# Block 14's halves copied on ScalarE behind the last one-hots; power ahead of the second gather; ranks, search steps, picks and weight parts at other steps

## The chip, the cores and the metric

The kernel runs on one core of a Trainium2 chip. The metric is device time in microseconds (us); the kernel before takes 1840.52 us (median of three runs, 1840.33 to 1842.64). The engines are TensorE (PE; PEld is its weight load), VectorE (DVE), ScalarE (ACT), GpSimd (POOL) and SyncE (SP), which only issues DMAs here. Each runs its instructions in program order and waits on semaphores for the others.

## The reference

```
lat = lat + g1 * ((gate_b * conv3(gate_c * v)) @ w_out)     # gate_b, gate_c, v = split(hl @ w_in)
h   = modulate(rms_norm(lat, norm_g[1]), sh2, sc2)          # 2048 tokens x 1024
aff = softmax(h @ w_router)                                 # 16 experts
g, idx = top_k(aff.T, 256)                                  # expert choice: 256 tokens an expert
hid = silu(h[idx] @ w_gate[e]) * (h[idx] @ w_up[e])
lat = lat + g2 * scatter_add(idx, (hid @ w_down[e]) * g)
```

There is one layer, in float32; a condition vector gives the shifts, scales and gates (sh, sc, g1, g2).

## The kernel before

All large products are split: each operand is rounded to a high part (`fp32r`) and a low part, the remainder, and PE adds three products (high x high, high x low, low x high). Of every weight piece of 512 KB, `split_high` (ACT, L267, 1.05 us) makes the high part and `split_low` (DVE, L277, 1.22 us) the low one; raw pieces come on SP's queue, and a raw buffer's next load is issued when its low part is done.

Tokens are worked on in 16 blocks of 128. Up to about 530 us the kernel computes the conditioning, the norm, the in-projection and the convolution. Then each block tb goes through the out-projection: eight steps k of `out_mm(tb + 1, k)` (L1217, L1218, L1220), and behind each step `behind(tb, k)` issues work of earlier blocks: residual and norm (`out_res`, L1232 and L1234), the second norm's output (`out_h2`, L1315), its transfer to memory as two 16-bit halves (`halves_out`, L1286), from which a DMA transpose makes the router's operand, the router's products (`router_mm`, `router_sum` L1387, for the last blocks `turn_xt` L1330 and `direct_mm` L1339), and the softmax (`router_sm`, L1397 to L1407).

In the same stretch the first expert's 256 tokens are found by ranks, so that its gather can begin before the last block is done. For block c, `row_turn` (L1445) turns its affinities into a row, `rank_a` compares it with all rows so far (`hits`, DVE L1456, and `equal`, POOL L1459 and L1460), `rank_b` counts on PE (L1466), and `rank_c` (DVE L1471) corrects the counts. After blocks 7 and 11 the ranked tokens are sorted and cut to 256 (`sort_a` L1475 and L1477, `sort_b` L1489, `sort_c`, `sort_d`, and a turn of `best`). `plan` lists at which (block, step, order within the step) each of these runs; steps with a negative third number run ahead of `behind_block`, the others after it. All the small PSUM tiles of these functions come from one pool, `tp`, which has two buffers that are handed out in turn; an allocation waits until the last reader of the tile two allocations earlier is done.

The last block (730 to 747 us) is written out by hand. `fetch_first` gathers the ranked tokens (POOL L1627, two gathers), `out_res_last` and `out_rms` norm the block (the power, POOL L1270), the softmax gives its affinities (logits L1399), PE turns `best` into a row (L1642) and the block's own values into another (L1654), DVE counts (L1657 to L1666) and makes the one-hots `chosen` (L1669, L1671), PE picks the columns of the first expert's operand (L1686, L1688) and turns the rest (L1693). `fill(n)` issues n matmuls whose result is not used. Block 14's halves are copied by POOL (L1284) and stored from POOL's queue (L1288).

The experts follow in the order gate_up(0), down(0), gate_up(1), down(1), gate_up(2), and from then on gate_up(e) and down(e - 1) by halves. A gate_up half has 8 steps k of 24 products of 256 columns (L1908), a down half 4 steps kk of 12 products of 512 columns (L1995 to L1997). Places are written (stage, expert, half, step, i): i = -1 is ahead of the weight splits of the step, 0 behind them, 1 in the middle of its products. The tables `SPLITS`, `HIGH`, `DOWN_SPLITS` and `DOWN_HIGH` say up to which weight piece low parts are made in a step and how many high parts more. `FEW_AT` places the rounds of the search for the threshold of expert 1 (PE L382 behind DVE L379), `ALL_AT` those for all experts (counts DVE L1713 and ACT L1717, PE L1724, DVE L1726 and L1730; one step joins the key's two parts, L1800), and `PICK_AT` the picks of experts 1 to 3: `pick_oh` makes one-hots (DVE L1821), `pick` multiplies them (PE L1829), copies the result out (DVE L1831) and gathers the tokens (POOL L1837); experts 1 and 2 are turned on PE by `turn_here` (L1879, its copies L1881 and L1882). After a gate_up half, ACT and DVE form the gated products (L1938, L1939, L1942).

Of the kernel before, what the change touches and what calls it, by code (L numbers as in the profile page):

```python
# [13 lines left out]
ALU = mybir.AluOpType  # L14
# [4 lines left out]
D = 1024  # L19
# [20 lines left out]
SPLITS = {(0, 0): (0, 1, 2, 3, 4, 6, 8, 10), (0, 1): (10, 11, 12, 13, 14, 15, 16, 18),  # L40
          (1, 0): (25, 27, 28, 29, 30, 32, 33, 34), (1, 1): (34, 35, 37, 38, 39, 40, 40, 41),
          (2, 0): (51, 52, 54, 55, 55, 57, 59, 60), (2, 1): (61, 62, 63, 64, 65, 67, 68, 69)}
HIGH = {(0, 0): (2, 2, 2, 2, 2, 2, 1, 1), (0, 1): (1, 1, 1, 1, 1, 1, 1, 1),
        (1, 0): (0, 0, 1, 0, 0, 0, 0, 0)}
DOWN_SPLITS = {(0, 0): (19, 19, 20, 21), (0, 1): (22, 24, 25, 25),
               (1, 0): (42, 43, 44, 46), (1, 1): (47, 48, 49, 50)}
DOWN_HIGH = {(0, 0): (1, 1, 1, 1), (0, 1): (1, 1, 1, 1),
             (1, 0): (1, 1, 1, 1), (1, 1): (1, 1, 1, 1)}
# [4 lines left out]
          ("g", 0, 1, 5, 1)]  # L53
ALL_AT = [("d", 0, 0, 1, 0), ("d", 0, 0, 2, 1), ("d", 0, 0, 3, 1), ("d", 0, 1, 0, 1), ("d", 0, 1, 1, 1),
# [3 lines left out]
PICK_AT = {1: (("g", 0, 1, 6, 0), ("g", 0, 1, 7, 0), ("d", 0, 0, 3, 0), ("d", 0, 1, 0, 0),  # L58
# [14 lines left out]
def block_kernel(ctx: ExitStack, tc, x, c, ada_w, ada_b, norm_g, w_in, conv, w_out, router, wg, wu, wd, out):  # L73
# [330 lines left out]
    with tc.tile_pool(name="mix", bufs=1) as mix, ExitStack() as ctx_mixd:  # L404
# [839 lines left out]
        def out_res_last(tb):  # L1244
# [7 lines left out]
            direct_mm(tb, 0)  # L1252
            pt = turn_xt(tb, 1, True, lambda: fill(2))
            fill(2)
            nc.vector.tensor_tensor(ss[:, 0:1], ss[:, 1:2], ss[:, 2:3], op=ALU.add)
            for j in (0, 2):
                nc.vector.tensor_copy(hx_of[tb][:, 4 + j:6 + j], pt[:, j:j + 2])
                if j == 0:
                    nc.vector.tensor_scalar(ss[:, 1:2], ss[:, 3:4], ss[:, 0:1], 1.0 / D, op0=ALU.add, op1=ALU.mult)
# [162 lines left out]
        def value(c, n=1):  # L1422
            return affh[:, c // 8, 0, c % 8:c % 8 + n]
# [85 lines left out]
        def plan():  # L1509
            for c, t, a, b, d in ((0, (5, 7), (6, 4), (6, 7), (6, 7, 6)), (1, None, (6, 7), (7, 3), (7, 4)),  # L1510
# [6 lines left out]
                early = -4 if c == 11 else 0  # L1517
                if t:
                    steps[(*t, 7)] = lambda c=c: row_turn(place(c), value(c, 1 if c else 4))
# [591 lines left out]
```

## Time and profile before

| | |
|---|---|
| median of three runs | 1840.52 us |
| profiled execution | 1838.64 us |
| its span | 1836.9 us |
| mean granted TensorE clock | 0.997 |

The profile is one execution. Its page gives the busy time of each engine, the queues, the chain that ended last and the costliest groups of instructions; the trace behind it can be read as lists of waits, as windows and as a timeline, in us from the span's start. In a timeline a row is: start, length, engine, line, operation, output <- input, shape, count; and in brackets the idle time of the engine before it and what released it. The granted clock is 1.00 at 2.4 GHz and 0.50 at 1.2 GHz.

### The profile page before, as it was taken

What the parts mean: (1) busy time and instruction counts of PE and PEld (TensorE: products, weight loads), DVE (VectorE), ACT (ScalarE), POOL (GpSimd) and SP (SyncE); (2) the same over time, 40 slices, a digit from 0 to 9 for tenths busy, and PEclk for the clock granted to TensorE, in tenths of its full rate; (3) what the DMA queues carried; (4) which work ended last, traced back from release to release, by engine and by line L of the source; (5) the groups of instructions that cost most, each with busy time, mean ns of one, the idle gap of its engine ahead of it and who ended that gap; (6) DMA issues with size and microseconds to landing.
All of it is one profiled execution on the core that took longest, in us unless ns stands there. A gap on an engine that the chain in (4) does not pass through costs nothing.

```text
span 1836.9 us, 29869 instructions
## 1 busy us (share of the span) xinstructions
PE 1799.5 (98%) x11588; PEld 1604.7 (87%) x11588; DVE 1282.7 (70%) x1855; ACT 912.0 (50%) x1274; POOL 371.0 (20%) x579
## 2 busy tenths in 40 slices
PE   7999999999999999999999999999999999999997
PEld 6788888887888777889899999999999999999996
DVE  6786878888867776777676666676576566666653
ACT  4665455333445554655465455455455445545541
POOL 2324201121111645222200210211121021021102
PEclk9999999999999999999999999999999999999999
DMA  9756565565589774666787887978878878787774
GB/s 338 245 174 212 170 227 183 161 162 136 147 259 293 222 212 146 232 184 198 222 257 218 256 233 224 265 214 243 261 225 238 241 252 230 230 255 227 234 225 81
DMA packets 306494, 401.09 MB, mean 218 GB/s; under 512 B 100004, under 2 KB 170960, under 8 KB 306352
## 3 DMA queue, kind: packets, MB, share of 16 engines
q1 hardware_dynamic: 280736, 307.91, 54.9%
q0 software_dynamic: 25616, 91.26, 17.0%
q8 instruction: 91, 1.49, 0.3%
q14 instruction: 51, 0.42, 0.1%
HBM read 316.27 MB, written 63.98 MB: 207 GB/s over the span
## 4 chain that ended last, share of the span: by engine, by line
PE 85%; DVE 6%; DMA 2%; ACT 2%; issue 2%; POOL 1%; SPq 0%; POOLq 0%; DVEq 0%; ACTq 0%
PE pm L1908 38%; PE pm L1995 6%; PE pm L1997 6%; PE pm L1996 6%; PE pm L920 5%; PE pm L922 5%; PE pm L921 5%; PE pm L1217 2%; PE pm L1218 2%; PE pm L1220 2%; PE pm L546 1%; PE pm L547 1%; PE pm L549 1%; DMA rows<-aw 1%; DVE sb L900 1%
## 5 line engine op out<-in xcount | busy, mean ns | idle before, releaser
L1908 PE MATMUL pm<-xT,ws 128*128 128x256 f32 x6144 | 712.2, 278 | 0.0
L1908 PEld LDWEIGHTS pm<-xT,ws 128*128 128x128 f32 x6144 | 708.9, 188 | 2.9 <-DVE ws L277 0.4
L277 DVE TENSOR_TENSOR ws<-raw,ws 128x1024 fp32r<-128x1024 f32 x389 | 462.4, 1221 | 259.3 <-ACT ws L267 259.1
L267 ACT ACTIVATE ws<-raw 128x1024 fp32r<-128x1024 f32 x389 | 393.7, 1053 | 386.9 <-PE pm L1908 271.2
L2031 POOL DMA_INDIRECT out_dram<-ot,idx x30 | 96.6, 3220 | 544.5 <-DVE ot L2020 540.5
L1995 PE MATMUL pm<-ws,hT 128*128 128x512 f32 x504 | 199.5, 396 | 0.0
L1997 PE MATMUL pm<-ws,hT 128*128 128x512 f32 x504 | 198.6, 394 | 0.0
L1996 PE MATMUL pm<-ws,hT 128*128 128x512 f32 x504 | 197.4, 392 | 0.0
L920 PE MATMUL pm<-tg,sb 128*128 128x512 f32 x472 | 184.7, 391 | 1.1 <-ACT cx L987 1.1
L922 PE MATMUL pm<-tg,sb 128*128 128x512 f32 x472 | 183.8, 389 | 0.0
L921 PE MATMUL pm<-tg,sb 128*128 128x512 f32 x472 | 183.7, 389 | 0.0
L900 DVE TENSOR_TENSOR sb<-raw,sb 128x512 fp32r<-128x512 f32 x144 | 98.9, 689 | 59.1 <-ACT sb L899 57.8
L899 ACT ACTIVATE sb<-raw 128x512 fp32r<-128x512 f32 x144 | 88.7, 625 | 65.7 <-DVE raw L908 14.6
L1997 PEld LDWEIGHTS pm<-ws,hT 128*128 128x128 f32 x504 | 95.0, 188 | 20.3
L1996 PEld LDWEIGHTS pm<-ws,hT 128*128 128x128 f32 x504 | 95.0, 188 | 19.6
L1995 PEld LDWEIGHTS pm<-ws,hT 128*128 128x128 f32 x504 | 94.9, 188 | 18.6
L920 PEld LDWEIGHTS pm<-tg,sb 128*128 128x128 f32 x472 | 88.6, 188 | 19.6 <-ACT cx L987 1.5
L922 PEld LDWEIGHTS pm<-tg,sb 128*128 128x128 f32 x472 | 88.6, 188 | 18.6
L921 PEld LDWEIGHTS pm<-tg,sb 128*128 128x128 f32 x472 | 88.6, 188 | 18.2
L1217 PE MATMUL pm<-ws,hl 128*128 128x512 f32 x256 | 104.2, 407 | 0.0
L1218 PE MATMUL pm<-ws,hl 128*128 128x512 f32 x256 | 100.0, 390 | 0.0
L1837 POOL DMA_INDIRECT xs<-hhalf,idx x26 | 37.8, 1456 | 260.1 <-issue 194.1
(453 smaller groups left out, 2365.6 us busy)
## 6 DMA issues: line engine op xcount, KB each, us to landing
raw<-in_moe_w_gate_dram SPq DMA_DIRECT2D x128, 512.0 KB, 5.0
raw<-in_moe_w_up_dram SPq DMA_DIRECT2D x128, 512.0 KB, 4.4
raw<-in_moe_w_down_dram SPq DMA_DIRECT2D x128, 512.0 KB, 4.6
raw<-in_sc_w_in_dram SPq DMA_DIRECT2D x42, 512.0 KB, 4.7
aw<-in_ada_w_dram POOLq DMA_DIRECT2D x32, 512.0 KB, 5.1
xt<-in_x_dram SPq DMA_DIRECT2D x31, 512.0 KB, 5.9
fu<-fscr SPq DMA_DIRECT2D x23, 512.0 KB, 4.9
hl<-in_ada_w_dram SPq DMA_DIRECT2D x32, 256.0 KB, 6.8
```

What stands on the lines that cost most here:

```text
L267: nc.scalar.activation(t[:, 0], raws[n_high], AF.Copy)
L277: (eng or nc.vector).tensor_sub(t[:, 1, ..., s], raw[..., s], t[:, 0, ..., s].bitcast(F32))
L900: nc.vector.tensor_sub(t[:, 1], full, t[:, 0].bitcast(F32))
L920: nc.tensor.matmul(o, t[:, 0, j], r[:, 0], start=(first and j == 0), stop=False, skip_group_check=True)
L921: nc.tensor.matmul(o, t[:, 1, j], r[:, 0], start=False, stop=False, skip_group_check=True)
L922: nc.tensor.matmul(o, t[:, 0, j], r[:, 1], start=False, stop=end, skip_group_check=True)
L1217: nc.tensor.matmul(ps[h], vh[:, k], w[:, 0, half(h)], start=(k == 0), stop=False)
L1218: nc.tensor.matmul(ps[h], vh[:, k], w[:, 1, half(h)], start=False, stop=False)
L1908: nc.tensor.matmul(o, w[:, i // 2, j, c0], xT[:, i % 2, k], start=(k == i == 0 and f % 2 == 0), stop=(k == KD - 1 and i == 2), skip_group_ ...
L1995: nc.tensor.matmul(ps[s], h, w[:, 0, j], start=(k == 0), stop=False)
L1996: nc.tensor.matmul(ps[s], h, w[:, 1, j], start=False, stop=False)
L1997: nc.tensor.matmul(ps[s], l, w[:, 0, j], start=False, stop=(k == KD - 1))
```

## The change

In the last block, `direct_mm(tb, 0)` takes the place of the filler between the two pairs of transposes, the second gather is issued behind the power and the sum of the sorted values, two fillers are shorter, and block 14's halves are copied on ScalarE and stored from SP's queue; the copy's place in program order stays behind the one-hots. The ranks and sorts get tables of places of their own, and several functions may share a place. The searches, the picks and the weight parts get other places in their tables.

```diff
-SPLITS = {(0, 0): (0, 1, 2, 3, 4, 6, 8, 10), (0, 1): (10, 11, 12, 13, 14, 15, 16, 18),
-          (1, 0): (25, 27, 28, 29, 30, 32, 33, 34), (1, 1): (34, 35, 37, 38, 39, 40, 40, 41),
+SPLITS = {(0, 0): (0, 1, 2, 3, 5, 7, 8, 10), (0, 1): (10, 10, 11, 12, 14, 15, 16, 19),
+          (1, 0): (25, 27, 28, 29, 29, 30, 32, 33), (1, 1): (34, 35, 37, 38, 39, 40, 40, 41),
...
-        (1, 0): (0, 0, 1, 0, 0, 0, 0, 0)}
...
+        (1, 0): (1, 2, 2, 1, 1, 1, 1, 2), (1, 1): (2, 1, 0, 0, 0, 0, 0, 0),
...
-               (1, 0): (42, 43, 44, 46), (1, 1): (47, 48, 49, 50)}
...
+               (1, 0): (45, 46, 46, 48), (1, 1): (50, 51, 51, 52)}
...
-          ("g", 0, 1, 5, 1)]
+          ("g", 0, 1, 7, -1)]
...
-          ("g", 1, 0, 1, -1), ("g", 1, 0, 2, -1), ("g", 1, 0, 3, -1), ("g", 1, 0, 4, -1), ("g", 1, 0, 4, 0),
-          ("g", 1, 0, 5, 0), ("g", 1, 0, 7, -1), ("g", 1, 1, 1, -1), ("g", 1, 1, 2, -1), ("g", 1, 1, 3, -1),
-          ("g", 1, 1, 4, -1), ("g", 1, 1, 4, 1), ("g", 1, 1, 5, -1), ("g", 1, 1, 5, 1), ("g", 1, 1, 6, -1)]
...
-           2: (("g", 1, 1, 7, 0), ("d", 1, 0, 0, 0), ("d", 1, 0, 3, -1), ("d", 1, 1, 0, -1),
-               ("d", 1, 1, 1, -1), ("d", 1, 1, 1, -1)),
...
+          ("g", 1, 0, 1, -1), ("g", 1, 0, 2, -1), ("g", 1, 0, 2, 1), ("g", 1, 0, 3, -1), ("g", 1, 0, 4, -1),
+          ("g", 1, 0, 4, 1), ("g", 1, 0, 6, 0), ("g", 1, 1, 1, -1), ("g", 1, 1, 2, -1), ("g", 1, 1, 3, -1),
+          ("g", 1, 1, 4, -1), ("g", 1, 1, 4, 1), ("g", 1, 1, 5, -1), ("g", 1, 1, 5, 0), ("g", 1, 1, 6, 0)]
...
+           2: (("g", 1, 1, 7, 1), ("g", 1, 1, 7, 1), ("d", 1, 0, 2, -1), ("d", 1, 0, 3, 1),
+               ("d", 1, 1, 1, 0), ("d", 1, 1, 1, 0)),
...
+RANK_AT = {0: ((5, 7, 7), (6, 0, 3), (6, 6, 3), (6, 7, 3)),
...
+           4: ((6, 7, 5), (8, 0, 0), (8, 6, 0), (8, 7, 3)),
+           5: ((7, 7, -3), (8, 7, 0), (9, 4, 3), (9, 5, 0)),
+           6: ((8, 7, 7), (9, 0, 3), (9, 6, 0), (9, 7, 5)),
+           7: ((10, 0, -3), (10, 2, -3), (10, 6, 5), (10, 7, -1)),
+           8: ((10, 7, 7), (11, 7, 3), (12, 1, -3), (12, 2, 2)),
+           9: ((11, 7, 5), (12, 4, 0), (12, 5, 6), (12, 6, 3)),
...
+SORT_AT = {7: ((11, 2, 0), (11, 5, -3), (11, 6, -3)),
+           11: ((13, 0, -0.5), (13, 4, -1), (13, 6, 3))}
...
             fill(4)
-            direct_mm(tb, 0)
-            pt = turn_xt(tb, 1, True, lambda: fill(2))
+            pt = turn_xt(tb, 1, True, lambda: direct_mm(tb, 0))
             fill(2)
...
-            for c, t, a, b, d in ((0, (5, 7), (6, 4), (6, 7), (6, 7, 6)), (1, None, (6, 7), (7, 3), (7, 4)),
...
-                                  (4, (6, 7), (8, 4), (8, 7), (8, 7, 6)), (5, (7, 7), (8, 7), (9, 3), (9, 4)),
-                                  (6, (8, 7), (9, 4), (9, 7), (9, 7, 6)), (7, (9, 7), (10, 4), (10, 7), (10, 7)),
...
+            for c, (t, a, b, d) in RANK_AT.items():
...
-                    steps.pop(t)()
+                    for f in steps.pop(t):
+                        f()
...
         fetch_first(1)
-        fetch_first(0)
         out_res_last(tb)
         out_rms(tb)
         sort_v(pk_c)
+        fetch_first(0)
...
-        fill(6)
+        fill(4)
...
-        fill(7)
+        fill(6)
...
-        halves_out(tb - 1, u_last[0], eng=nc.gpsimd)
+        halves_out(tb - 1, u_last[0])
```

In `RANK_AT` the four places of a block are those of `row_turn`, `rank_a`, `rank_b` and `rank_c`; in `SORT_AT` the three are those of `sort_a`, of `sort_b` with `sort_c` and `sort_d`, and of the turn of `best`.

## Rows read from the trace of the kernel before

**Rows 1.** The page's first part: busy time of each engine, its share of the span, and instructions.

```profile
PE 1799.5 (98%) x11588; PEld 1604.7 (87%) x11588; DVE 1282.7 (70%) x1855; ACT 912.0 (50%) x1274; POOL 371.0 (20%) x579
```

**Rows 2.** The list of PE's waits: tile and line, what released it, then us in total, times, and the longest.

```profile
PE pt L1879 <- DMA xs<-hscr,idx: 3.4, 1, 3.4
...
PE pc L1724 <- ACT hit L1717: 2.4, 1, 2.4
```

**Rows 3.** Windows: stretch, its length, busy time and instructions of PE, PEld, DVE, ACT and POOL, the granted clock, the share of the DMA engines and GB/s. The stretches are that of the last one-hots, that behind a search round, and that behind the third expert's gather.

```profile
738.00:742.00 4.00, 2.60 (x14) 1.81 (x14) 3.50 (x11) 1.59 (x3) 3.41 (x9) 1.00 0.89 348
...
836.70:839.00 2.30, 2.30 (x13) 2.30 (x13) 1.41 (x2) 1.81 (x2) 0.00 (x0) 0.52 0.56 195
...
883.80:885.00 1.20, 1.19 (x5) 1.20 (x6) 0.00 (x0) 0.06 (x1) 0.00 (x0) 0.50 0.65 249
```

**Rows 4.** The chain that ended last, in order of time: the products of one gate_up half in the later experts.

```profile
1079.45 21.79 PE pm L1908 x192
```

**Rows 5.** The timeline of the last block.

```profile
734.35 0.98 POOL L1627 DMA_INDIRECT xs<-hscr,idx  x1 [0.27 <-POOL idx L1625]
...
735.36 0.87 POOL L1270 TENSOR_TENSOR rstd<-ss,mhalf 128x1 f32<-128x1 f32 x1
...
739.49 0.29 DVE L1669 TENSOR_SCALAR chosen<-slot_r,n_last 128x128 f32<-128x128 bf16 x1
739.54 1.98 POOL L1284 COPY uh<-u 128x2048 uint16<-128x2048 uint16 x1
...
739.88 1.73 DVE L1671 TENSOR_SCALAR chosen<-slot_r,n_last 128x128 f32<-128x128 bf16 x1
...
741.66 0.49 PE L1686 MATMUL pm<-chosen,xs 128*128 128x128 f32 x2 [1.40 <-DVE chosen L1671]
...
745.34 1.04 PE L1693 MATMUL pt<-identf,xs 128*128 128x128 f32 x8
```

**Rows 6.** Two answers on one tile and one line: how long the two gathers of the last block took from issue to landing, and the duration of ScalarE's copies of halves in the earlier blocks (ns, least, median and most).

```profile
DMA to landing us min/median/max: 5.6/6.6/7.7
...
L1286 ACT ACTIVATE hl<-u x14: 1893/1896/1913, 539.0 to 712.8; 128x2048 uint16<-128x2048 uint16 x14
```

**Rows 7.** The timeline of the first gate_up stage, at two rounds of the search for one expert.

```profile
768.68 0.28 PE L382 MATMUL pc<-each,sameq 128*128 128x32 f32 x1 [0.36 <-DVE each L379]
...
775.62 0.28 PE L382 MATMUL pc<-each,sameq 128*128 128x32 f32 x1 [0.68 <-DVE each L379]
```

**Rows 8.** The timeline of the second expert's gate_up, at rounds of the search over all experts: a round's product, its last count, the product that waited, and the products behind it.

```profile
829.19 0.17 PE L1724 MATMUL pc<-cnt,same 128*128 128x4 f32 x1
...
830.91 0.19 ACT L1717 ACTIVATION_READ_ACCUMULATOR hit<-keys,nb 128x1 fp32r x1
...
834.61 0.27 PE L1724 MATMUL pc<-cnt,same 128*128 128x4 f32 x1 [2.40 <-ACT hit L1717]
834.75 4.60 PE L1908 MATMUL pm<-xT,ws 128*128 128x256 f32 x24
```

**Rows 9.** The timeline of the third expert's pick and gather, and, without a time in front, how long from issue to landing the gathers of this expert took and then those of the expert before.

```profile
868.47 2.49 DVE L1821 TENSOR_TENSOR oh<-slot_r,row 128x512 bf16<-128x512 bf16 x4
...
871.48 0.56 PE L1829 MATMUL pi<-ax,oh 128*128 128x10 bf16 x16
...
875.43 0.16 DVE L1831 COPY pk<-pi 128x10 f32<-128x10 f32 x1
...
876.59 1.54 POOL L1837 DMA_INDIRECT xs<-hscr,idx  x1 [19.25 <-DVE gate L1844]
...
878.43 0.96 POOL L1837 DMA_INDIRECT xs<-hscr,idx  x1 [0.30 <-issue]
...
883.82 1.09 PE L1879 MATMUL pt<-identf,xs 128*128 128x128 f32 x4 [3.42 <-DMA xs<-hscr,idx]
...
DMA to landing us min/median/max: 7.1/7.7/8.4
...
DMA to landing us min/median/max: 5.3/5.3/5.3
```

**Rows 10.** The blocks with ranks. First the timeline: starts of a block on VectorE (L1232), the first and the last of the nine places, a compare, the norm's output, and a count on PE. Then a group of instructions by line (busy us, mean ns, idle time before them and its releaser), and, last, who waited for L1471 (us, times).

```profile
601.35 0.68 DVE L1232 TENSOR_TENSOR u<-pm,g1b 128x512 f32<-128x512 f32 x1
...
614.49 0.68 DVE L1232 TENSOR_TENSOR u<-pm,g1b 128x512 f32<-128x512 f32 x1
...
636.97 0.32 PE L1445 MATMUL pt<-identf,aff 128*128 128x128 f32 x1 [0.47 <-DVE aff L1407]
...
642.41 0.68 DVE L1232 TENSOR_TENSOR u<-pm,g1b 128x512 f32<-128x512 f32 x1
...
648.98 1.19 DVE L1456 SCALAR_TENSOR_TENSOR hits<-ranked,zero,aff 128x896 bf16<-128x896 f32 x1
...
650.23 0.30 PE L1466 MATMUL pr<-ones_b,hits 128*128 128x1 bf16 x6
...
651.27 1.41 DVE L1315 SCALAR_TENSOR_TENSOR u<-u,rstd,sh2b 128x512 f32<-128x512 f32 x2
...
679.55 0.32 PE L1445 MATMUL pt<-identf,aff 128*128 128x128 f32 x1 [0.27 <-DVE lg L1397]
...
L1308 DVE TENSOR_TENSOR hl<-hl 128x1024 fp32r<-128x1024 f32 x5 | 6.1, 1226 | 5.9 <-ACT hl L1303 5.9
...
  PE pt L1330: 0.2, 1
```

More of the change, by code (lines that the diff above doesn't have):

```diff
@@ L39 @@
 SORTS = (0, 8, 12)
-SPLITS = {(0, 0): (0, 1, 2, 3, 4, 6, 8, 10), (0, 1): (10, 11, 12, 13, 14, 15, 16, 18),
-          (1, 0): (25, 27, 28, 29, 30, 32, 33, 34), (1, 1): (34, 35, 37, 38, 39, 40, 40, 41),
-          (2, 0): (51, 52, 54, 55, 55, 57, 59, 60), (2, 1): (61, 62, 63, 64, 65, 67, 68, 69)}
-HIGH = {(0, 0): (2, 2, 2, 2, 2, 2, 1, 1), (0, 1): (1, 1, 1, 1, 1, 1, 1, 1),
-        (1, 0): (0, 0, 1, 0, 0, 0, 0, 0)}
-DOWN_SPLITS = {(0, 0): (19, 19, 20, 21), (0, 1): (22, 24, 25, 25),
-               (1, 0): (42, 43, 44, 46), (1, 1): (47, 48, 49, 50)}
-DOWN_HIGH = {(0, 0): (1, 1, 1, 1), (0, 1): (1, 1, 1, 1),
-             (1, 0): (1, 1, 1, 1), (1, 1): (1, 1, 1, 1)}
+SPLITS = {(0, 0): (0, 1, 2, 3, 5, 7, 8, 10), (0, 1): (10, 10, 11, 12, 14, 15, 16, 19),
+          (1, 0): (25, 27, 28, 29, 29, 30, 32, 33), (1, 1): (34, 35, 37, 38, 39, 40, 40, 41),
+          (2, 0): (52, 54, 56, 56, 56, 56, 59, 59), (2, 1): (61, 63, 63, 63, 64, 65, 67, 68)}
+HIGH = {(0, 0): (2, 2, 2, 2, 2, 3, 1, 1), (0, 1): (1, 1, 0, 0, 2, 2, 2, 2),
+        (1, 0): (1, 2, 2, 1, 1, 1, 1, 2), (1, 1): (2, 1, 0, 0, 0, 0, 0, 0),
+        (2, 0): (0, 0, 1, 0, 0, 1, 1, 1), (2, 1): (1, 1, 1, 1, 0, 0, 0, 0)}
+DOWN_SPLITS = {(0, 0): (20, 20, 21, 21), (0, 1): (21, 24, 25, 25),
+               (1, 0): (45, 46, 46, 48), (1, 1): (50, 51, 51, 52)}
+DOWN_HIGH = {(0, 0): (1, 2, 2, 2), (0, 1): (2, 2, 2, 3),
+             (1, 0): (0, 0, 0, 0), (1, 1): (0, 0, 0, 0)}
 N_GROUP = 7
@@ L1251, in out_res_last @@
             fill(4)
-            direct_mm(tb, 0)
-            pt = turn_xt(tb, 1, True, lambda: fill(2))
+            pt = turn_xt(tb, 1, True, lambda: direct_mm(tb, 0))
             fill(2)
             nc.vector.tensor_tensor(ss[:, 0:1], ss[:, 1:2], ss[:, 2:3], op=ALU.add)
[L1256 to L1259, printed above, removed]
+            nc.vector.tensor_copy(hx_of[tb][:, 4:6], pt[:, 0:2])
+            nc.vector.tensor_scalar(ss[:, 1:2], ss[:, 3:4], ss[:, 0:1], 1.0 / D, op0=ALU.add, op1=ALU.mult)
+            nc.vector.tensor_copy(hx_of[tb][:, 6:8], pt[:, 2:4])
         def out_rms(tb):
@@ L1509, in plan @@
         def plan():
-            for c, t, a, b, d in ((0, (5, 7), (6, 4), (6, 7), (6, 7, 6)), (1, None, (6, 7), (7, 3), (7, 4)),
[6 rows of a table removed]
-                early = -4 if c == 11 else 0
-                if t:
-                    steps[(*t, 7)] = lambda c=c: row_turn(place(c), value(c, 1 if c else 4))
-                steps[(*a, 5)] = lambda c=c: rank_a(c)
-                steps[(*b, early + c % 2)] = lambda c=c: rank_b(c)
-                steps[(*d, early + 2 + c % 2) if len(d) == 2 else d] = lambda c=c: rank_c(c)
-            for c, a, b, d in ((7, (11, 2), (11, 4), (11, 6)), (11, (13, 0), (13, 2), (13, 6))):
-                steps[(*a, -0.5 if c == 11 else 4)] = lambda c=c: sort_a(c)
-                steps[(*b, 6)] = lambda c=c: (sort_b(c), sort_d(sort_c()))
-                steps[(*d, 6)] = lambda: row_turn(0, best)
+            for c, (t, a, b, d) in RANK_AT.items():
+                if t:
+                    steps.setdefault(t, []).append(lambda c=c: row_turn(place(c), value(c, 1 if c else 4)))
+                steps.setdefault(a, []).append(lambda c=c: rank_a(c))
+                steps.setdefault(b, []).append(lambda c=c: rank_b(c))
+                steps.setdefault(d, []).append(lambda c=c: rank_c(c))
+            for c, (a, b, d) in SORT_AT.items():
+                steps.setdefault(a, []).append(lambda c=c: sort_a(c))
+                steps.setdefault(b, []).append(lambda c=c: (sort_b(c), sort_d(sort_c())))
+                steps.setdefault(d, []).append(lambda: row_turn(0, best))
         plan()
```

2 lines of the change are left out of this document (1 added, 1 removed), and 16 rows, old and new, of tables (PICK_AT, RANK_AT, steps).

## The prediction

> **What bounds the kernel now.** I read the busy shares first. TensorE (PE) is busy for 1799.5 of 1836.9 us, 98%, and no other engine passes 70% of its own time besides PE's weight loads [rows 1]. So only two things can be gained: stretches in which PE stands still, and the stretches behind them in which its clock is lower. In the expert loop there is nothing of the kind: each half of a gate-and-up stage is 192 products in 21.78 us, 0.1134 us each [rows 4], and the change leaves everything from the fourth expert on as it is. The list of PE's waits is read next. The three long ones that the change touches are a gather for the third expert (L1879, 3.4 us), a search round (L1724, 2.4) and the last block's one-hot (L1686, 1.4) [rows 2, 5]. The windows by granted clock come last: behind the 1.40 us wait the clock is still 1.00, behind the two longer ones it is at 0.50 to 0.52 [rows 3], that is 1.2 in place of 2.4 GHz, so a matmul takes twice as long until it rises again. A wait of 2.4 us or more therefore costs more than itself here, one of 1.4 us does not.
>
> The sum below is made against the profiled execution, 1838.64 us (span 1836.9). The median of the runs shown is 1840.52, 1.9 us longer; I add that back at the end.
>
> **1. Tail of the last block: -2.1 us (-1.0 to -2.6).** Before, the power (L1270) starts at 735.36, just behind the second gather on the same queue (L1627 at 734.35, 0.98 us), and the logits, the softmax, the row of own values and the counts follow in a chain [rows 5]. The new order puts the power ahead of that gather, and the last transposes no longer sit behind four routers' products and two fillers; what the power then waits for (the two sums of squares) is there some 0.8 us earlier. Dropping two of six and one of seven filler matmuls keeps PE from arriving late at the row of own values. I take the count chain 1.05 us earlier.
> The second gain is at the one-hots. L1669 takes 0.29 us; L1671, the same operation on the same shapes, takes 1.73 and ends at 741.61, with GpSimd's copy of block 14's halves (L1284, 1.98 us from 739.54) ending at 741.52 [rows 5]. With that copy on ScalarE, L1671 should take 0.29: 1.44 us less. Together PE could start L1686 at 741.66 - 1.05 - 1.44 = 739.15, 2.5 earlier. The copy itself costs 1.9 us on ScalarE [rows 6], from about 738.9 to 740.8. What hides it are the products from L1686 to L1693, 3.7 us on PE [rows 5]: their first slices may be drained up to 0.7 later, the last, for which the first gate-and-up stage waits, come well behind it. Without that cover it would cost about 0.5 us. The store of the halves moves to SP's queue, where the weight loads are; none is due until the first parts of gate-and-up are used, so I price it at nothing.
> What is late next is the second gather: it issues near 736.3 in place of 734.35. The two gathers took 5.6 and 7.7 us to land [rows 6], so it lands at 741.9 to 744.0, and its first use (L1693) moves from 745.34 to 742.85. A wait of 0 to 1.1; I take 0.4, as the same bytes are moved in the same stretch. -2.5 + 0.4 = -2.1.
>
> **2. The search for one expert's threshold, in the first gate-and-up stage: -1.0 us (-0.2 to -1.3).** Two rounds stop PE because the small product before them (L379) queues behind a weight split on VectorE: idle 0.36 at 768.68 and 0.68 at 775.62 [rows 7]. The new tables move a weight part behind each of them. Elsewhere in that stage one part now stands ahead of a round; I price that at a few tenths, about what the restart of PE adds to the two waits. Net the two gaps, 1.04.
>
> **3. The search over all experts: -2.0 us (-3.0 to -0.5).** One round's trip from its product to the last count took 829.19 to 831.10, 1.9 us; with a key step in between, and only 12 products to cover it, PE stood 2.40 us at 834.61, and the next 24 products took 4.60 us in place of 24 x 0.1134 = 2.72 [rows 4, 8]. Together 4.3. The new places give each of three rounds 12 products of cover, 1.36 us. That leaves 0.55 and 0.45 for two plain rounds and 1.0 to 1.3 for the one with the key step, 2.0 to 2.3 in all, each shorter than the 1.40 that left the clock alone [rows 3]. 4.3 - 2.3 = 2.0.
>
> **4. The third expert's pick and gather: -3.9 us (-4.3 to -2.5).** The pick's product ended at 872.04, but its copy out (L1831) ran only at 875.43, because in program order it stood behind the gate's products on VectorE and a split; the gather issued at 876.59 and took 7.1 us to land, and L1879 started at 883.82 after an idle 3.42 us [rows 9]. At half clock for 3.4 us this costs about 1.6 more: 5.0 in all [rows 3, 9]. Now the pick stands before those products. It waits for the last one-hot: 868.47 + 2.49 = 870.96 before [rows 9], a little earlier now (the high weight parts ahead of it are copied sooner), so the product costs PE a stall of 0.6; the count of prefixes ahead of it, now a step nearer to its product, I put at 0.35, between nothing and a plain round's 0.55. The gather issues near 872.0. Its transposes are one k pair earlier, near 877.7. The gathers here took 7.1 and 8.4 us beside weight loads; those of the expert before 5.3 [rows 9]. There is less load in flight at 872 than at 877, so I take 5.3 to 6: landing at 877.3 to 878, a stall of 0 to 0.3. -5.0 + 0.95 + 0.15 = -3.9. With 7.1 the stall is 1.4 and the gain 2.5.
> The gather's issue took 1.54 us at 876.59, beside a weight split on VectorE, and 0.96 at 878.43 [rows 9]: 0.6 us that would come on top if a split or the gate's products run beside it at 872 too. The Trainium skill, page SBUF — State Buffer, section Who interferes with whom, has a rule that speaks against the change here: a VectorE instruction with two SBUF inputs shuts out a GpSimd instruction that reads SBUF for its whole length. By that rule the gather would start up to one split later and the gain here would be 3.3 instead of 3.9; the two issue times agree with it. I leave it within the range.
>
> **5. Ranks in blocks 6 to 12: +0.9 us (-3.8 to +5).** Gains first. In the stretch of the old compares (L1456, up to 1.19 us) VectorE delays the router's softmax, so that the turns of the affinities wait; nine such places, from the one at 636.97 to that at 679.55, lose 3.8 us in all, by the start of each matmul against that of the one before, less its own length [rows 10]. The new table moves compares into VectorE's two idle stretches of a block (5.9 us in five before L1308, 1.18 each, and one like it before L1115), and VectorE, which took 13.1 us for the block from 601.35 to 614.49 and 14.0 for each of the next two (to 642.41) [rows 10], should keep 13.1. I take all 3.8.
> The cost: the rank count of block 6 (L1466) moves from step 7 to step 6 of block 9. Its PSUM tile comes from a pool of two that turns, routers' sums and counts share; the tile two allocations earlier is that of block 5's count, released by L1471, which now stands behind the softmax and the two L1315 of that block on VectorE. In the block shown these end at 651.27 + 1.41 = 652.7, that is 10.3 after the block's start at 642.41, 9.1 without the compare between [rows 10]. At 13.1 a block it starts at 640.7, so the release comes at 649.8. PE was at the old place at 650.23; without 1.1 of waits (those of the nine that lie ahead of it) and one step of 13.1 / 8 = 1.64 earlier it arrives at 647.5. Stall 2.3. That the pool can hold PE up is seen once: L1330 waited for L1471 0.2 us [rows 10]. From below the cost is nothing (if the tile is another, or the count comes before the softmax), from above 3 us. A stall of 2.3 lies between 1.40 (clock kept) and 2.40 (clock halved); the nearer is 2.40, so I add 1.7 for half a clock. Block 9's count moves to right behind its compare, of which 0.65 stays uncovered (a compare takes up to 1.19). 2.3 + 1.7 + 0.65 - 3.8 = +0.9.
>
> **Sum.** -2.1 - 1.0 - 2.0 - 3.9 + 0.9 = -8.1: a profiled execution of 1830.5, and with the 1.9 between profile and median 1832.4.
>
> **The rivals.**
> *A: the forecast, 1832.4.* Chance 0.47.
> *B: no stall at block 9, or none that drops the clock.* For it: only one wait on this pool is seen before. Against it: the order of the allocations. 1830.7 without the drop, 1828.4 without the stall. 0.25.
> *C: the expert gains are half as large.* The rounds are only spread (term 3 at -0.5), the gather lands as late as before relative to its use (term 4 at -2.5), the chosen rows wait for the late gather (term 1 at -1.0): 1.5 + 1.4 + 1.1 = 4 us less, 1836.4. For it: gathers of 7.1 to 8.4 us; against it: the loads that made them so are later now. 0.19.
> *D: slower.* Place: the pool of two PSUM tiles in blocks 6 to 9. If the moved compares don't fit VectorE's idle stretches and it still lags by 2 us and more per two blocks, the stall at block 9 is 3 us longer (5.3, and 7.0 with 1.7 of clock), and four more counts and sums with margins under 1 us wait too, about 4.3 together, while the 3.8 stays: 7.0 + 4.3 + 0.65 = 11.9 against -9.0 of the other terms, +2.9: 1843.4; up to 1846 if a second wait drops the clock. It decides from a lag of about 1 us per block on. For it: VectorE lost 0.9 a block; against it: its idle before L1308 is as long as a compare. 0.07.
> *E: the change does not do what it says:* L1671 stays at 1.73 because another GpSimd instruction takes the copy's place, or ScalarE's copy delays xT as much as it frees. Then term 1 is nothing: 1834.5. 0.02 by itself.
>
> **How the numbers follow.** About 0.2%, 3.7 us, is what a measurement of this kernel can tell from no change: faster means below 1836.84, slower above 1844.20. A, B and E are faster, C in two cases of three (0.87 together); D is same or slower in equal parts. I take some from the first for what I don't see: faster 0.80, same 0.14, slower 0.06. The range 1827 to 1839 takes in A, B, C and E and leaves out D.
>
> **What would show it.** Right: L1671 near 0.3 us and L1686 near 739; L1879 without a wait of 2 us and the clock at 1.00 behind it; no round idle over 1.5; L1466 of block 6 with a wait of 2 us on L1471 near 647. Wrong: the gather landing past 880, L1693 waiting for the second gather, VectorE's blocks still 14 us, or several L1466 and L1387 waiting on tiles.

## The result, and the profile after

The changed kernel takes 1828.37 us (median of four runs, 1826.49 to 1831.57), the kernel before 1840.94 in the same comparison: a ratio of 0.9932 with a 95% interval of 0.9915 to 0.9949, so 9.4 to 15.7 us faster. The forecast was 1832.4 us, 8.1 less. The profiled execution took 1829.19 us (span 1827.4), 9.45 less than that of before, and stands 0.8 above its median, where that of before stood below its own.

Single executions scatter by 2 us and more, and the trace shows where: the first product of the out-projection starts anywhere from 513.0 to 516.7 us in the thirteen profiled executions of this study, whose code up to there is the same, and the first half of the blocks, which ends at the 129th product, takes 95.5 to 97.1 us. Nearly all of those 1.6 us lie in the products 17 to 48, ahead of the first rank that was moved. Behind that the same code repeats to 0.1 us in most traces, and to 0.3 us in the experts of e7, but for one thing (the last section). So the parts of the change are read from four stretches, each the difference of two starts in the timeline: *ranks* is from the 129th to the 253rd product of the out-projection (L1217 before, L1233 after), *tail* from there to the first product of the experts, *expert 1* and *expert 2* are the first two experts' gate_up and down stages, start to start. (Lines moved by 16 in the out-projection, 14 in the ranks, and 8 in the tail and the experts.)

| stretch, us | before | after | difference | forecast |
|---|---|---|---|---|
| ranks | 116.59 | 115.32 | -1.3 | +0.9 |
| tail | 19.40 | 17.00 | -2.4 | -2.1 |
| expert 1 | 74.01 | 72.97 | -1.0 | -1.0 |
| expert 2 | 80.09 | 73.21 | -6.9 | -5.9 |
| sum | 290.09 | 278.50 | -11.6 | -8.1 |

The page's first part after shows the same picture as [rows 1], with 2.4 us less of PE's busy time (five instructions fewer, and less time at the lower clock):

```profile
PE 1797.1 (98%) x11583; PEld 1600.8 (88%) x11583; DVE 1281.7 (70%) x1855; ACT 914.5 (50%) x1275; POOL 373.2 (20%) x577
```

The list of PE's waits after, columns as in [rows 2]. The gather of 3.4 us and the one-hot are gone from it; the rounds are three short waits in place of one long one; and of the new ones the longest is the second last line here (another, 0.3 us, stands at the count of block 9):

```profile
PE pc L1732 <- ACT hit L1725: 1.3, 3, 0.8
...
PE pt L1459 <- POOL best L1515: 1.0, 1, 1.0
PE pr L1480 <- POOL equal L1474: 0.8, 1, 0.8
PE pr L1480 <- ACT ws L283: 0.6, 1, 0.6
```

The timeline of the last block after, against [rows 5]. The power (L1284) no longer follows the second gather; that (L1635) starts behind it, at 737.17. Both one-hots take 0.29 us, and PE is at its first chosen product at 740.02; counted from the 253rd product that is 2.4 earlier than before. The transposes of the late gather (L1701) don't wait for it:

```profile
735.26 1.07 PE L1353 MATMUL pm<-rtA,hx 128*128 128x16 f32 x8
...
735.42 0.57 POOL L1284 TENSOR_TENSOR rstd<-ss,mhalf 128x1 f32<-128x1 f32 x1 [0.93 <-DVE ss L1272]
...
736.44 0.23 DVE L1413 SCALAR_TENSOR_TENSOR lg<-pm,rstd,lshift 128x16 f32<-128x16 f32 x1 [0.18 <-PE pm L1353]
...
737.17 1.28 POOL L1635 DMA_INDIRECT xs<-hscr,idx  x1 [0.34 <-POOL idx L1633]
...
739.29 0.29 DVE L1677 TENSOR_SCALAR chosen<-slot_r,n_last 128x128 f32<-128x128 bf16 x1
...
739.67 0.29 DVE L1679 TENSOR_SCALAR chosen<-slot_r,n_last 128x128 f32<-128x128 bf16 x1
739.69 1.89 ACT L1300 ACTIVATE uh<-u 128x2048 uint16<-128x2048 uint16 x1
...
740.02 0.49 PE L1694 MATMUL pm<-chosen,xs 128*128 128x128 f32 x2
...
741.60 0.33 SPq L1302 DMA_DIRECT2D hhalf<-uh  x1
...
742.02 0.85 SPq L258 DMA_DIRECT2D raw<-in_moe_w_up_dram  x1
...
743.69 1.04 PE L1701 MATMUL pt<-identf,xs 128*128 128x128 f32 x8
```

The last SP rows are something that the forecast had not seen: two weight loads that before left SP at 733.6 and 734.1 now stand behind the store of the halves (L1302) in SP's order and leave at 742.0 and 742.9. The two gathers land in 4.5 to 5.6 us, where [rows 6] have 5.6 to 7.7.

The third expert's pick after, against [rows 9]: its product runs at 865.31, its copy out 0.8 us later, the gather issues at 867.24, lands 4.4 to 5.4 us later by its line's answer, and the turn (L1887) at 872.88 waits for nothing. In the window behind it the clock is 1.00, where it was 0.50.

```profile
865.31 0.75 PE L1837 MATMUL pi<-ax,oh 128*128 128x10 bf16 x16
...
866.09 0.17 DVE L1839 COPY pk<-pi 128x10 f32<-128x10 f32 x1 [0.35 <-PE pi L1837]
...
867.24 1.05 POOL L1845 DMA_INDIRECT xs<-hscr,idx  x1 [14.71 <-PE pm L1916]
...
872.88 0.60 PE L1887 MATMUL pt<-identf,xs 128*128 128x128 f32 x4
```
```profile
872.00:878.00 6.00, 6.00 (x32) 4.97 (x31) 4.57 (x5) 3.04 (x5) 0.00 (x0) 1.00 0.89 312
```

### The profile page after: what moved, and what is told of

Read it like the earlier page. It is cut to its first block, busy times and chain, and to the rows that moved or that the text cites. A ratio compares the mean times of both kernels' runs of the same rounds, so it can differ in the third digit from the quotient of the medians.

```text
span 1827.4 us, 29857 instructions
## 1 busy us (share of the span) xinstructions
PE 1797.1 (98%) x11583; PEld 1600.8 (88%) x11583; DVE 1281.7 (70%) x1855; ACT 914.5 (50%) x1275; POOL 373.2 (20%) x577
## 4 chain that ended last, share of the span: by engine, by line
PE 58%; DVE 1%; POOL 0%; issue 0%; ACT 0%; POOLq 0%; DVEq 0%; ACTq 0%
PE pm L1916 38%; PE pm L2003 6%; PE pm L2005 6%; PE pm L2004 6%; PE pi L1837 0%; DVE ws L293 0%; PE pt L1887 0%; POOL out_dram L2039 0%; PE pm L1258 0%; ACT hit L1725 0%; POOL neg L1741 0%; PE pm L1694 0%; PE pm L1353 0%; POOLq L2115 0%; PE pm L1696 0%
## 5 line engine op out<-in xcount | busy, mean ns | idle before, releaser
L1233 PE MATMUL pm<-ws,hl 128*128 128x512 f32 x256 | 104.8, 409 | 0.2 <-ACT hl L1130 0.2
```

What stands on the lines that cost most here:

```text
L1233: nc.tensor.matmul(ps[h], vh[:, k], w[:, 0, half(h)], start=(k == 0), stop=False)
```

## The experiments

All start from the changed kernel, and none leaves out any of the computation. The table gives the stretches of each profiled execution, in us, and the ratio to the kernel before where there was more than one execution. The new places of the picks of experts 1 and 3 and of the last round of the first search were not undone by themselves.

| run | ranks | tail | expert 1 | expert 2 | ratio, 95% interval |
|---|---|---|---|---|---|
| changed kernel | 115.32 | 17.00 | 72.97 | 73.21 | 0.9932 (0.9915 to 0.9949) |
| e1 the same again | 115.31 | 16.99 | 72.97 | 73.27 | 0.9940 (0.9923 to 0.9956) |
| e2 halves on GpSimd | 115.31 | 17.00 | 72.90 | 73.29 | 0.9946 (0.9929 to 0.9963) |
| e3 gather ahead of the power | 115.24 | 17.29 | 72.92 | 73.27 | 0.9947 (0.9931 to 0.9964) |
| e4 pick 2 at its old places | 115.29 | 18.37 | 72.86 | 82.68 | 0.9988 (0.9978 to 0.9997) |
| e5 both tail pieces old | 115.28 | 19.02 | 72.91 | 73.31 | 0.9950 (0.9931 to 0.9969) |
| e6 search of all, old places | 115.28 | 17.00 | 72.99 | 75.61 | 0.9937 (0.9920 to 0.9953) |
| e7 ranks, old places | 116.53 | 18.38 | 73.22 | 73.52 | 0.9947 (0.9931 to 0.9964) |
| e8 correction behind next count | 116.25 | 18.38 | 73.03 | 73.29 | one execution |
| e9 weight parts old | 115.27 | 17.00 | 75.32 | 73.09 | one execution |
| e10 remaining waits | 111.59 | 17.86 | 73.02 | 72.90 | 0.9918 (0.9901 to 0.9935) |
| e11 remaining waits, mended | 112.50 | 16.94 | 73.36 | 71.42 | 0.9909 (0.9893 to 0.9926) |

**e1: the changed kernel again.** No edit.

> The changed kernel once more, beside the others. My theory says that its stages come out as in its first trace: from the first product of the out-projection to the one 252 later 207.65 us (before 208.09), from there to the first product of the experts 21.0 us (before 23.4), and from there to the first gate-and-up half of the fourth expert 226.0 us (before 234.0), each within 0.4 us; what the whole time scatters by more than that lies ahead of the out-projection. The rival, that the gain of the stages is itself scatter, has one of them off by 1 us or more.

The four stretches of the table came out within 0.1 us. The first figure of the expectation did not: it is 208.25 us against 207.65, outside the 0.4 that I had allowed, because it takes in the first half of the blocks, where the second block alone (products 17 to 32) took 0.6 longer with the same code. (This expectation's first two figures, and the 21.0 us of e3's, are counted to the 249th product, 4.0 us ahead of the 253rd.) The whole time (1829.15 us median) scatters with what lies ahead of the four stretches. Differences of 0.3 us in *ranks* and *tail*, and of some 0.5 in the experts, can be read from one profile, which the times alone, with intervals of 3 us on either side, can't give.

**e2: the halves on GpSimd.**

```diff
-        halves_out(tb - 1, u_last[0])
+        halves_out(tb - 1, u_last[0], eng=nc.gpsimd)
```

> Block 14's halves are copied and stored by GpSimd again, all else as changed. If VectorE's second one-hot was slow because GpSimd was copying, it takes 1.7 us again in place of 0.29, the first chosen product starts 1.3 to 1.5 us later, the weight loads leave SP near 734 instead of 742 and the gathers take 6 to 8 us instead of 4.5 to 5.6; the whole costs 1.4 to 2.0 us. If the tail was shortened by the earlier power alone, the one-hot stays near 0.3 us or the chosen products start where they do now, within 0.3 us.

My first expectation failed: the tail is 17.00, unchanged. The timeline shows why. GpSimd's queue holds the late gather and the casts of the gate now, so it reaches the copy only after VectorE has made the one-hot:

```profile
738.51 0.28 DVE L1679 TENSOR_SCALAR chosen<-slot_r,n_last 128x128 f32<-128x128 bf16 x1
...
739.59 1.88 POOL L1298 COPY uh<-u 128x2048 uint16<-128x2048 uint16 x1
```

The weight loads did leave SP at 733.2 and 733.7 again, and both gathers took 6.0 us to land. The late gather, issued at 736.01, landed by 742.1, still ahead of its first use at 742.53. It cost nothing, so those loads' new place is worth nothing either.

**e3: the second gather ahead of the power.**

```diff
         fetch_first(1)
+        fetch_first(0)
         out_res_last(tb)
         out_rms(tb)
         sort_v(pk_c)
-        fetch_first(0)
```

> The second gather is issued ahead of the power again, all else as changed. If the queue behind that gather held the power, the power starts 0.6 to 0.9 us later and the chosen products with it, so the tail is 0.6 to 0.9 us longer. If the transposes that now come sooner were what moved the chain, the power starts at most 0.2 us later and the tail keeps its 21.0 us.

Both halves were half right. The power starts 0.7 us later, counted from the 253rd product, as the first theory has it, but the tail is only 0.3 longer: in the changed kernel the logits (L1413) wait for PE's router products (L1353) anyway, and the power is done 0.3 us before these. Here they wait for the power:

```profile
731.51 1.07 PE L1353 MATMUL pm<-rtA,hx 128*128 128x16 f32 x8
...
732.35 0.60 POOL L1284 TENSOR_TENSOR rstd<-ss,mhalf 128x1 f32<-128x1 f32 x1
...
732.99 0.23 DVE L1413 SCALAR_TENSOR_TENSOR lg<-pm,rstd,lshift 128x16 f32<-128x16 f32 x1 [0.48 <-POOL rstd L1284]
```

The one-hot stayed at 0.29 with ScalarE copying.

**e5: both at once** (the two edits above together).

> Both old pieces of the tail at once: the second gather ahead of the power, and block 14's halves copied and stored by GpSimd; all else as changed. Each alone left the second one-hot at 0.29 us and the tail (from the 253rd product of the out-projection to the first of the experts) within 0.3 us of 17.0. My theory now is that only the two together put GpSimd's copy beside the one-hot: it takes 1.5 us or more, and the tail is 18.3 to 19.2 us. The rival, that the one-hot of before was slow for another reason, leaves it near 0.3 us and the tail at 17.3.

The tail is 19.02, 2.0 longer, and the one-hot takes as long as the copy beside it:

```profile
737.09 2.00 DVE L1679 TENSOR_SCALAR chosen<-slot_r,n_last 128x128 f32<-128x128 bf16 x1
737.12 1.89 POOL L1298 COPY uh<-u 128x2048 uint16<-128x2048 uint16 x1
...
739.15 0.49 PE L1694 MATMUL pm<-chosen,xs 128*128 128x128 f32 x2 [1.66 <-DVE chosen L1679]
```

So 1.7 of the tail's 2.4 us hang on the copy not running beside the one-hot, and either piece of the change is enough for that. The Trainium skill, page SBUF — State Buffer, section Who interferes with whom, says that VectorE's two-port modes, which tensor_scalar can enter, and a GpSimd instruction hold the shared port pair against each other for a whole instruction; 2.00 us beside the copy and 0.28 to 0.29 without it agree.

**e4: the pick of the third expert at its old places.**

```diff
-           2: (("g", 1, 1, 7, 1), ("g", 1, 1, 7, 1), ("d", 1, 0, 2, -1), ("d", 1, 0, 3, 1),
-               ("d", 1, 1, 1, 0), ("d", 1, 1, 1, 0)),
+           2: (("g", 1, 1, 7, 0), ("d", 1, 0, 0, 0), ("d", 1, 0, 3, -1), ("d", 1, 1, 0, -1),
+               ("d", 1, 1, 1, -1), ("d", 1, 1, 1, -1)),
```

> The third expert's one-hots, pick and turns at the places of before, all else as changed. By my theory the copy of the pick stands behind the gate's products and the weight splits again, the gather issues 4 us or more later, PE waits 3 us or more at the first turn, the clock falls to 0.50 behind it, and the stretch from the first product of the experts to the fourth expert is 4 to 9 us longer than 226.0 (above 5 if the splits that the new tables put at the start of that down stage are ahead of the copy). By the rival, that the new weight tables had freed the gather by themselves, it is at most 2 us longer.

Expert 2 takes 9.4 us more, twice what the old place cost in the kernel before (4.5, by the difference drawn under e6), and the whole kernel is back within 0.2% of the kernel before. (Its tail, 18.37, is not the edit's doing: see the last section.) The copy out now stands behind the gate's products and every weight split that the new tables put at the head of that stage, and runs at 874.13, 6.8 us after its product (866.76 + 0.56); the gather issues at 875.28 and the turn waits 7.50:

```profile
874.13 0.16 DVE L1839 COPY pk<-pi 128x10 f32<-128x10 f32 x1
...
875.28 1.55 POOL L1845 DMA_INDIRECT xs<-hscr,idx  x1 [22.63 <-DVE gate L1852]
...
883.18 1.09 PE L1887 MATMUL pt<-identf,xs 128*128 128x128 f32 x4 [7.50 <-DMA xs<-hscr,idx]
```
```profile
883.20:887.00 3.80, 3.80 (x11) 3.18 (x12) 2.06 (x3) 2.49 (x3) 0.00 (x0) 0.50 0.02 8
```

The second fence is the window behind the wait, at the clock's lower level, as in [rows 3]. The edit moves the whole pick and not the copy alone, but the rows show where the time goes: the copy waits for its turn on VectorE. With the pick moved ahead, the weight parts behind it cost it nothing: the changed kernel and e9, which has the parts of before, differ by 0.1 us in expert 2.

**e6: the search over all experts at its old places.**

```diff
-          ("g", 1, 0, 1, -1), ("g", 1, 0, 2, -1), ("g", 1, 0, 2, 1), ("g", 1, 0, 3, -1), ("g", 1, 0, 4, -1),
-          ("g", 1, 0, 4, 1), ("g", 1, 0, 6, 0), ("g", 1, 1, 1, -1), ("g", 1, 1, 2, -1), ("g", 1, 1, 3, -1),
+          ("g", 1, 0, 1, -1), ("g", 1, 0, 2, -1), ("g", 1, 0, 3, -1), ("g", 1, 0, 4, -1), ("g", 1, 0, 4, 0),
+          ("g", 1, 0, 5, 0), ("g", 1, 0, 7, -1), ("g", 1, 1, 1, -1), ("g", 1, 1, 2, -1), ("g", 1, 1, 3, -1),
...
```

> The rounds of the search over all experts at the places of before, all else as changed. My theory: two rounds stand next to each other again with 12 products of cover, one PE wait of about 2.4 us with the granted clock near 0.5 behind it, and gate-and-up and down of the second expert take 75.3 to 76.3 us in place of 73.2. The rival, that the new weight tables shorten the rounds as well (no weight split between them), has a wait under 1.5 us, no fall of the clock, and less than 1 us more.

Expert 2 takes 2.4 us more (75.61), one wait of 2.40 is back, and the window behind it is at 0.80 on average:

```profile
829.30 0.27 PE L1732 MATMUL pc<-cnt,same 128*128 128x4 f32 x1 [2.40 <-ACT hit L1725]
```
```profile
829.30:832.00 2.70, 2.69 (x18) 2.70 (x19) 1.98 (x6) 1.81 (x5) 1.84 (x2) 0.80 0.25 96
```

Of expert 2's 6.9 us, then, 2.4 come from the rounds, and the other 4.5, by difference, from the pick. In time the difference doesn't show (0.9937 against 0.9932 and 0.9940): it takes the trace.

**e7: the ranks at their old places.** `plan` and `behind` as before the change.

> The ranks and sorts of blocks 5 to 14 at the places of before, all else as changed. My theory: the turns of the affinities wait behind the compares again (0.6, 0.9 and 0.4 us near 637, 651 and 680) and the stretch from the 129th to the 253rd product of the out-projection takes 116.6 us in place of 115.3. The rival: the stretch is within 0.3 us of 115.3, since what the new places gain they lose at other counts.

116.53 against 115.3: the 1.2 us are the ranks' places. The list of PE's waits between 600 and 700 us has the turns of the affinities back, with the numbers of before:

```profile
PE pt L1459 <- DVE aff L1421: 1.2, 2, 0.7
PE pt L1459 <- DVE lg L1411: 0.3, 1, 0.3
```

**e8: block 5's correction behind block 6's count.**

```diff
-           5: ((7, 7, -3), (8, 7, 0), (9, 4, 3), (9, 5, 0)),
+           5: ((7, 7, -3), (8, 7, 0), (9, 4, 3), (9, 6, 3)),
```

> The correction of block 5's count, which reads its PSUM tile, is moved behind the count of block 6 in program order (from the fifth to the sixth step of block 9); nothing else changes. I had reckoned that block 6's count takes the tile of block 5's count and so must wait for this correction. If the pool gives the tile that was released first in program order (the router's sum), the move changes nothing: the count of block 6 starts with no wait on it, the stretch stays within 0.2 us of 115.3. If the tiles went strictly in turn, the count could not run before the correction at all.

The count of block 6 (six hits, then the equal) runs at its place, 4.6 us before the correction that I had thought it must wait for, so it doesn't take that tile. What follows it does: the next turn waits 0.81 for the correction, and the stretch is 0.9 longer, not unchanged as I had expected.

```profile
647.20 0.30 PE L1480 MATMUL pr<-ones_b,hits 128*128 128x1 bf16 x6
...
648.30 0.18 PE L1480 MATMUL pr<-ones_b,equal 128*128 128x1 bf16 x1 [0.79 <-POOL equal L1474]
...
651.84 0.42 DVE L1485 TENSOR_TENSOR count<-count,pr 128x6 f32<-128x6 f32 x2
652.14 0.29 PE L1459 MATMUL pt<-identf,aff 128*128 128x128 f32 x1 [0.81 <-DVE count L1485]
```

So the two tiles don't go strictly in turn, though I said so above of this pool. Since there are two, the count must have the tile of the router's sum. What fits both runs is a pool that hands out the tile whose last reader comes first in program order; no other order was tried.

**e9: the weight parts as before.** The four tables `SPLITS`, `HIGH`, `DOWN_SPLITS`, `DOWN_HIGH`.

> The four tables of weight parts as before, all other places as changed. My theory: the waits of the first expert's search (0.4 and 0.7 us behind a weight split) come back in part, so the first expert's stage (its first product to that of the second expert) takes 73.5 to 74.1 us in place of 72.97; the second expert's stage stays within 0.7 us of 73.25, because the pick's gather issues at the same place with fewer splits ahead. The rival, that the third expert's gather lands in time only since the weight parts moved too, has a wait at its first turn of 1 us or more and the stage at 74.5 us or more.

Expert 1 is 2.4 us longer, more than the 0.5 to 1.1 that I expected (and more than all that the change gained there). The two waits of the first search (L397) are back, and with the new one of the changed kernel (L398 there, 0.4) gone, the gate-and-up stage is 1.0 longer, as expected. The rest, 1.4, I had not expected: it comes in the down stage behind it, where PE now waits 0.6 for a round of the search over all experts (L1731). The rounds of that stage stand where they did before the change; what moved there is expert 1's pick, and with the old parts a weight part (L292) and a copy of the picked tokens (L1889) now stand on VectorE between a round's product, at 808.07, and its next step (L1733), at 810.00. Expert 2 stays at 73.09, so the third expert's gather owes nothing to the weight parts. The first two lines are the list of waits up to 818 us, in expert 1; the third is that of both stages, and its other three waits, 1.3 us, are expert 2's, as in the changed kernel:

```profile
PE pc L397 <- DVE each L394: 1.1, 2, 0.7
PE pc L1731 <- ACT hit L1724: 0.6, 1, 0.6
...
PE pc L1731 <- ACT hit L1724: 1.9, 4, 0.8
```

**e10: the waits that remain.**

```diff
-          ("g", 1, 0, 1, -1), ("g", 1, 0, 2, -1), ("g", 1, 0, 2, 1), ("g", 1, 0, 3, -1), ("g", 1, 0, 4, -1),
-          ("g", 1, 0, 4, 1), ("g", 1, 0, 6, 0),
+          ("g", 1, 0, 1, -1), ("g", 1, 0, 2, -1), ("g", 1, 0, 3, -1), ("g", 1, 0, 4, -1), ("g", 1, 0, 5, -1),
+          ("g", 1, 0, 6, -1), ("g", 1, 0, 7, -1),
...
-           6: ((8, 7, 7), (9, 0, 3), (9, 6, 0), (9, 7, 5)),
+           6: ((8, 7, 7), (9, 0, 3), (9, 7, 0), (9, 7, 5)),
...
-           9: ((11, 7, 5), (12, 4, 0), (12, 5, 6), (12, 6, 3)),
+           9: ((11, 7, 5), (12, 4, 0), (12, 6, 0), (12, 6, 3)),
...
-           11: ((13, 0, -0.5), (13, 4, -1), (13, 6, 3))}
+           11: ((13, 0, -0.5), (13, 4, -1), (13, 7, -3))}
...
+        fill(2)
         p_row = mm.tile([P, P], F32, name="pm", tag="mm")
...
-        fill(4)
+        fill(5)
```

(With it, block 13's count goes one step later and the first half's weight parts are those of before.)

> The changed kernel with five of its remaining waits taken on: the search rounds of the second expert at seven successive steps; two rank counts one half-step or step later, a turn of the sorted values one step later, and the count of block 13 one step later; the weight parts of the very first half as before; one filler more and two ahead of the turned row. My theory, that each of these waits is only a matter of its place: the stretch of the out-projection falls from 115.3 to about 112.8 us (0.98, 0.7 and up to 1.2 gone), the tail is 16.4 to 17.0 without a fall of the clock, the first expert's stage 72.4 and the second's 71.5 (1.8 us of round waits gone): about 5 us in all, near 1823. The rival: the waits come back at the next reader of the same tile or the next round, and less than 2 us is left.

The out-projection's gain came (111.59 + 17.86 is 2.9 less than 115.32 + 17.00, the 0.8 of block 13's count having only moved from the one to the other), those of expert 1 (73.02, where I had expected 72.4) and expert 2 did not. In expert 2, with a round at the head of each step, VectorE makes the step's weight part behind the round, and the products wait for it:

```profile
833.75 2.45 PE L1917 MATMUL pm<-xT,ws 128*128 128x256 f32 x19 [1.55 <-DVE ws L293]
```

**e11: the same, mended.** Block 13's count is back in its place, and the weight parts are those below, shown against the changed kernel. Against e10 the first expert's first half differs too, by its last low part, which goes to the next half:

```diff
-SPLITS = {(0, 0): (0, 1, 2, 3, 5, 7, 8, 10),
-          (1, 0): (25, 27, 28, 29, 29, 30, 32, 33),
+SPLITS = {(0, 0): (0, 1, 2, 3, 4, 6, 8, 9),
+          (1, 0): (25, 27, 28, 29, 30, 31, 32, 33),
...
-HIGH = {(0, 0): (2, 2, 2, 2, 2, 3, 1, 1),
-        (1, 0): (1, 2, 2, 1, 1, 1, 1, 2),
+HIGH = {(0, 0): (2, 2, 2, 2, 2, 2, 1, 2),
+        (1, 0): (1, 2, 2, 1, 0, 0, 1, 2),
```

> The run before, mended at two places: the count of block 13 is back where the changed kernel has it (moving it only moved its wait from one stretch to the next), and the second expert's weight parts are made one in each step of its first half, so that the round that now heads each step holds none back that the next products need. My theory: the two stretches of the out-projection and its tail together stay 2.9 us below the changed kernel's 132.3, and the second expert's stage falls from 72.9 to 71.2 to 71.6 us, the 1.7 us wait for a weight part gone; about 4.5 to 5 us below the changed kernel, near 1823.5. The rival: the weight parts, made earlier, hold back the rounds on VectorE or ScalarE, waits of rounds come back, and the second expert's stage stays above 72.5.

Expert 2 fell to 71.42, as expected; expert 1 rose by 0.4 over the changed kernel's (and 0.3 over e10's), since the wait of a search round behind the weight splits moved on to another round (0.7 us at L398). The four stretches together take 274.2 us, 4.3 less than the changed kernel's 278.5, and the kernel 1823.21 us against 1840.35 of before in the same comparison: the best of this study by its stretches, though its interval overlaps with those of e10 and of the changed kernel.

## Why the prediction was right, and where it was not

**The sum** was 3.5 us short in the four stretches (-11.6 for -8.1), most of it in term 5. That the profiled execution came within 1.3 us of its forecast (1829.19 for 1830.5) is in part luck: what lies outside the four stretches took 2.1 us longer in it than in that of before, nearly all of it in the scatter up to the 129th product. And the 1.9 us that I added back between profile and median was the scatter of one execution, not an offset; this time the profile stands 0.8 above its median. By medians the forecast is 4.0 us off, 2.7 of them from there.

**The bound** held: all that was taken apart is a wait of PE or a stretch at the lower clock behind one, and the later experts' stages did not move (21.78 and 21.79 us for 192 products, as [rows 4]).

**Term 1, the tail** (-2.1, measured -2.4). The sum was near, one of its two reasons half right. I gave 1.05 us to the earlier power and 1.44 to the copy on ScalarE, as if they added up from separate causes. e2, e3 and e5 show one cause of 1.7 us, the one-hot beside GpSimd's copy, that either piece removes; what the power's place alone is worth with the copy on ScalarE is 0.3 (e3). The rest, about 0.4 (2.4 - 2.0), was not taken apart; the shorter fillers and the new order of the transposes are what is left for it. The wait for the late gather, 0.4 in my sum, did not come. The weight loads, which I had said were not due, moved behind the store on SP, and the gathers landed sooner; but in e2, with the loads at their old time, the gather was in time as well. The -2.4 is itself one outcome of two: in three executions of seven this tail takes 18.4 us, which is 1.0 less than the one of before that was profiled (the last section).

**Term 2, the first search** (-1.0, measured -1.0). Right in size, and by e9 it is the weight parts that carry it: without them both waits are back, 0.4 and 0.7. The loss that I put elsewhere in that stage came too (L398, 0.4 us).

**Term 3, the rounds** (-2.0, measured -2.4 by e6). Right: three waits of 0.25 to 0.78 instead of one of 2.40, and no fall of the clock. I had misread which rounds have the 12 products of cover: the one with the key step, which I had priced at 1.0 to 1.3, has a whole step of 24 and waits for nothing, and the three that do wait are plain ones.

**Term 4, pick and gather** (-3.9, measured -4.5 by difference). The mechanism was right and the size too small: the gather took 4.4 to 5.4 us to land, where I took 5.3 to 6, and the pick's own product, for which I had priced a stall of 0.6, took 0.75 us in place of 0.56. The 0.6 more for issues beside VectorE came in part, at the second of them, and cost PE nothing: they took 1.05 and 1.39 us, where the quickest had 0.96. (For a landing of 7.1 us my own terms give a gain of 2.65, not the 2.5 that I wrote.)

**Term 5, the ranks** (+0.9, measured -1.3 by e7). This is the step that failed, and it is the error of the sum: 2.2 of the 3.5 us between -8.1 and -11.6. I had block 6's count wait 2.3 us for the tile of block 5's count, with 1.7 of lower clock behind it. It did not take that tile; e8 shows it, and that the tile of the router's sum, released earlier in program order, is the one left for it. In its place PE waits 0.8 us for GpSimd's `equal` at the same count (the row in the list of waits above), and the clock stays at 1.00. The count of block 9, for which I had 0.65, has a wait of 0.3, and the 16 products around it (the 209th to the 224th) take 0.7 longer than before, 14.99 us for 14.28; with that count half a step later, in e10, they take 14.19. The gain held in kind: VectorE keeps 13.1 us a block, as forecast (L1248 starts at 603.31 and, three blocks on, at 642.69). Of the 3.8 us of old waits, only the 1.5 at the turns of the affinities stand in the list of waits, and those are gone, as their group between 600 and 700 us shows (the last figure is the idle time before them; e7 has 1.5 there):

```profile
L1459 PE MATMUL pt<-identf,aff 128*128 128x128 f32 x10 | 2.6, 281 | 0.0
```

From the 129th product to the 205th the new places are 2.2 us ahead of the old ones; to the 253rd it is 1.3, so 0.9 is given back in the last blocks, most of it at the count of block 9.

Rival B (no stall in block 9) is thus near what happened in the ranks, with a little more gained in the experts than I had given. That its figure, 1828.4, is the measured median is luck: it has the same 1.9 in it. C and D did not: no gather came late, and no second wait on a tile. E, that moving the copy does nothing, is true of that piece by itself and false of the change.

## What to carry to other kernels

Where an operation has two causes of delay that overlap, price them together: undo both before saying what either is worth. A small copy that frees a long transfer belongs ahead of the bulk work on its engine, and the earlier that bulk work is allowed to run, the more a late copy costs (4.5 us before, 9.4 with the new weight parts). When whole runs scatter by more than the effect, compare starts of the same instruction in two traces, stretch by stretch.

## What the runs showed that I had not expected

The clock in the changed tail is not certain. Seven executions ran exactly this tail; in four (after, e1, e6, e9) it took 17.0 us, in three (e4, e7, e8) 18.4. Their instructions are the same, but behind two short idle stretches of PE (0.3 us at L1650 and up to 0.2 at L1662) the granted clock falls to 0.50 in these three for 3.4 us. The window of e4:

```profile
738.60:740.00 1.40, 1.40 (x4) 1.04 (x4) 0.88 (x2) 1.40 (x2) 1.26 (x4) 0.50 0.84 304
```

So my reading that a wait of 1.4 us or less leaves the clock alone [rows 3] is too simple. What lets it fall in some executions and not in others is not shown. A run of 16-column products (L1353) lies ahead of these stretches, but that can't be all: in the kernel before the same products were followed by a longer wait, as in e3 and e5 (0.85 us in each), and the clock stayed at 1.00 in the one profiled execution of each of these. The row of before:

```profile
736.73 0.32 PE L1642 MATMUL pm<-identf,best 128*128 128x128 f32 x1 [0.85 <-POOL best L1501]
```

Whether the fall came with the change, by its shorter fillers or otherwise, is therefore open. The two executions with the fillers of e10 and e11 in those gaps kept the clock at 1.00; whether that holds in every execution was not tried.
